# A hybrid decoder trunk in split fp32: each half-head's scores placed 24 or 28 steps behind the issue of their query and key loads instead of 3, and those loads 6 steps behind their stores instead of 1

## The chip, the cores and the metric

The kernel runs on one core of one Trainium2 chip. The metric is the device time of one execution in microseconds (us): 2202.98 us, the median of 3 runs (2202.58 to 2203.88). Lower is better.

## The reference

One decoder layer (sequence 1024, width 2048), float32 in and out. One input projection feeds eight differential-attention heads and eight recurrent blocks; their gated outputs go through one output projection.

```
h = rms_norm(x, norm_gain);  proj = h @ w_in          # [1024, 2048] @ [2048, 6144]
q, k, v, g_attn, xr, g_rec = split(proj)
q, k = rope(q), rope(k)                               # 8 heads x 2 maps x 64
...                                                   # per 128 query rows, causal:
  p = softmax(mask(q_m . k_m / 8))  for m = 0, 1
  w = p[0] - lam * p[1];  o = w @ v                   # 8 heads x 128
o = rms_norm(o, subln_gain) * silu(g_attn)
r = rg_lru(causal_conv(xr)) * silu(g_rec)             # 8 blocks x 128, a scan over the sequence
x = x + concat(o, r) @ w_out;  out = rms_norm(x, final_gain)
```

## The kernel before

The sequence is worked off in two halves of 512 tokens (`b`, and `l` where attention speaks of the half). Every dense product is done in three matmuls on a high and a low part of each operand (`triple`, L363: weight high by data high, weight high by data low, weight low by data high). A weight tile of 128 x 512 is loaded by SP, rounded into its high part on ACT (L169) and subtracted into its low part on POOL or DVE (L170); it serves four triples. The units of a half are taken in the order of `UNITS` (L56): a head is four projections of 16 triples each (two for queries and keys, one for values, one for the gate), a recurrent block two.

All other work runs beside this stream as Python generators in `Slots` (L64). Their clock, `now`, advances by one step after each triple, so a step is 3 matmuls of PE, and `yield n` puts the rest of a generator n steps further down the stream. That sets the program's order by hand; the framework's scheduler then moves single instructions on each engine's queue. Each engine, SP included, takes its own queue in order.

The path that the change touches is that of a head's queries and keys:
- `head` (L422) multiplies the two projections with the rotary tables on DVE; `rope` (L459) adds them, splits the results into high and low parts, and 4 steps later stores four tiles to `fs` in HBM (L155, `fs<-b`, each 4x32x512, 256 KB). One step later it marks the head ready.
- `loader` (L608) then calls `head_load` (L584), which reads the head back in another layout, all on SP: the new half's two key tiles (128x512) and four query tiles, each of 64 rows fetched twice (128x1x512). In the second half of the sequence it also loads the first half's two key tiles and the two value tiles `vs`.
- `scores` (L656) waits until the head is in `hd`, then 3 steps more, and runs `score` (L617) for four blocks of 128 queries, 10 steps apart. One block is, for each of the two maps, L632 (query high) and L633 (query low) into the accumulator `sw`, twice where the keys exceed 512; then the masked maximum on DVE (L637), the exponentials on ACT (L644), and the weighted difference on DVE (L652). `weighted` (L676) transposes the result on PE (L755) and multiplies it with the values (L777 to L780).

The tiles `b` are 89 slots that are given out in the order in which they come free (`alloc`, `rel`); a load into a slot waits for the slot's last reader.

Of the kernel before, what the change touches and what calls it, by code (L numbers as in the profile page):

```python
# [55 lines left out]
UNITS = ("h0", "h1", "r0", "h2", "r1", "h3", "r2", "h4", "r3", "h5", "r4", "h6", "h7", "r5", "r6",  # L56
         "r7")
ORDER = (0, 1, 2, 3, 4, 8, 9, 10, 11, 12, 5, 6, 13, 14, 7, 15)
SCORE_STEP = 2
SCORE_PACE = (4, 4)  # L60
TURN_PACE = 2
# [2 lines left out]
class Slots:  # L64


    def __init__(self):
        self.now = 0
        self.seq = 0
        self.tasks = []  # L70
# [36 lines left out]
class Trunk:  # L107
    def __init__(self, ctx, tc, io):
        self.tc = tc
        self.nc = tc.nc  # L110
        self.io = io
        e = ctx.enter_context
        self.cst = e(tc.tile_pool(name="cst", bufs=1))
        self.dram = e(tc.tile_pool(name="scr", bufs=1, space=bass.MemoryType.DRAM))
        self.bp = e(tc.tile_pool(name="buf", bufs=1))
        self.ps = e(tc.tile_pool(name="ps", bufs=1, space=bass.MemoryType.PSUM))
        self.tr, self.av, *self.dense = [
            self.ps.tile([P, HALF], F32, name=f"pq{i}") for i in range(4)]
        self.swide = [self.ps.tile([P, 1024], F32, name=f"sw{i}") for i in range(2)]
        self.n = 0  # L120
        self.sl = Slots()
        self.free = deque(range(NB))
        self.wide = [self.bp.tile([P, 1024], F32, name=f"wide{i}") for i in range(5)]
        self.avbusy = self.trbusy = False
        self.cur = self.phase = 0
        self.rsb, self.sin, self.cos, self.tabs, self.Y = {}, {}, {}, {}, {}
        self.fs, self.vsc, self.vnow, self.gate, self.rgate, self.msc = {}, {}, {}, {}, {}, {}
        self.ready, self.hd, self.es = set(), {}, {}
        self.scored, self.flipped, self.weighed = [], 0, 0

    def nm(self, s):
# [110 lines left out]
    def weights(self):  # L242
        io = self.io
        for b in range(2):
# [7 lines left out]
            yield from (io["w_in"][u, g] for u in us for g in range(4))  # L252
            yield from (io["w_out"][cg, kt] for cg in range(4) for kt in ORDER)

# [204 lines left out]
    def rope(self, b, h, ts):  # L459
        nc = self.nc  # L460
        t1, t2, t3, t4 = ts
        self.tt(t1.f, t1.f, t2.f, ALU.subtract)
        self.tt(t3.f, t3.f, t4.f, ALU.add)
        yield 1
        self.split(t1.f, t2, t1)
        self.split(t3.f, t4, t3)
        yield 4
        fs = self.dram.tile([4, 4, 32, HALF], F32, name=self.nm("fs"))
        for i, t in enumerate((t2, t4, t1, t3)):
            self.load(fs[:, i], t.f)  # L470
        self.rel(*ts)
        self.fs[h, b] = fs
        yield 1
        self.ready.add(("q", h, b))

    def values(self, b, h, vt):
# [107 lines left out]
    def head_load(self, h, l):  # L584
        k, q, v = [], [], []
        for c in range(l + 1):
            ks = []
            for m in range(2):
                kk = self.allocr()
                self.load(kk.f, self.fs[h, c][2 + m].rearrange("i r c -> (i r) c"))  # L590
                ks.append(kk)
            k.append(ks)
        for i in (0, 2):
            for m in range(2):
                t = self.allocr()
                src = self.fs[h, l][m, i:i + 2].rearrange("i r c -> (i r) c")
                self.load(t.f, src.unsqueeze(0).broadcast_to([2, 64, HALF]))
                q.append(t)
        if l:
            vs = []  # L600
            for d in self.vsc[h]:
                t = self.allocr()
                self.load(t.f, d)
                vs.append(t)
            v.append(vs)
        self.hd[h, l] = (k, q, v)

    def loader(self):  # L608
        for l in range(2):
            for h in range(NH):  # L610
                while (("q", h, l) not in self.ready or 8 * l + h - self.weighed > 1
                       or len(self.free) < FREE_HEAD):
                    yield 1
                self.head_load(h, l)
                yield 1

    def score(self, h, l, j, p0, es):  # L617
# [8 lines left out]
        for m in range(2):  # L626
            st = self.swide[m]
            for c in range((cols + 511) // 512):
# [4 lines left out]
                nc.tensor.matmul(o, lhsT=q[2 + m].r[:, qs], rhs=kk, start=False, stop=True)  # L633
        yield SCORE_STEP
        for m in range(2):
# [4 lines left out]
        nc.vector.tensor_scalar_mul(mx, mx, -(QK ** -0.5))  # L640
        yield SCORE_STEP
        p1 = self.wide[3]
        for m, p in enumerate((p0, p1)):
            nc.scalar.activation(p[:, :cols], self.swide[m][:, :cols], AF.Exp, scale=QK ** -0.5,  # L644
                                 bias=mx[:, m:m + 1], accum_out=sm[:, m:m + 1])
        yield SCORE_STEP
        nc.vector.tensor_tensor(out=es[:, j:j + 1], in0=sm[:, 0:1], in1=sm[:, 0:1], op=ALU.mult)
# [8 lines left out]
    def scores(self):  # L656
        n = 0
        for l in range(2):
            for h in range(NH):
                while (h, l) not in self.hd:  # L660
                    yield 1
                yield 3
                es = self.cst.tile([P, 4], F32, name=self.nm("es"), tag="es", bufs=4)
                self.es[h, l] = es
                for j in range(4):
                    while n - 2 * self.flipped > 3:
                        yield 1
                    p0 = self.wide[(0, 1, 2, 4)[n % 4]]
                    n += 1
                    yield from self.score(h, l, j, p0, es)  # L670
                    self.scored.append(p0)
                    yield SCORE_PACE[l]
                k, q, v = self.hd[h, l]
                self.rel(*q, *(t for ks in k for t in ks))
# [118 lines left out]
    def outputs(self, b):  # L793
# [10 lines left out]
        for cg in range(4):  # L804
            for i, kt in enumerate(ORDER):
                while cg == 0 and len(raws) + len(mixes) < min(KT, i + 5):
                    raws.append(self.mix(ORDER[len(raws) + len(mixes)], b))
                while cg == 0 and len(mixes) < min(KT, i + 2):
                    x, hi, lo = raws.popleft(), self.allocr(), self.allocr()
                    mixes[ORDER[len(mixes)]] = (hi, lo)  # L810
                    self.split(x.f, hi, lo)
# [55 lines left out]
            self.rel(y)  # L867

    def run(self):
        engines = {mybir.EngineType.PE, mybir.EngineType.SP}  # L870
        if True:
            self.consts()
            for gen in (self.stream(), self.loader(), self.scores(), self.weighted()):
                self.sl.spawn(gen)
            for b in range(2):
                for name in UNITS:
                    (self.head if name[0] == "h" else self.rec)(b, int(name[1]))
                self.final(b)
                self.outputs(b)
# [58 lines left out]
```

## Time and profile before

| what | value |
|---|---|
| median of 3 runs | 2202.98 us |
| the profiled execution | 2201.42 us |
| its span, first to last instruction | 2199.6 us |
| PE busy | 1739.8 us, 79% |
| POOL, ACT, DVE busy | 858.7, 793.6, 761.4 us |
| mean granted TensorE clock | 0.883 |
| DMA, mean rate | 108 GB/s |

The profile gives each engine's busy time and, for each group of instructions, the idle time just before them and what ended it. TensorE has two clock levels, 1.2 and 2.4 GHz; a granted clock of 1.00 in a stretch is the higher, 0.50 the lower. Idle time of an engine costs something only where the end of the program hangs on that engine.

### The profile page before, as it was taken

Reading aid. Unit: us, or ns where it says so; the run is one execution under the profiler, and the core shown is the slowest. Engines: PE = TensorE matmul, PEld = TensorE weight load, DVE = VectorE, ACT = ScalarE, POOL = GpSimd, SP = SyncE. Lnnn points to the kernel's source line nnn. Section 1 sums busy time; section 2 is a strip of 40 time slices with the busy share of each in tenths; the row PEclk is TensorE's granted clock in tenths of the full one; section 3 lists DMA queues with packets and bytes.
Section 4 is the critical chain, followed back from the end, with each engine's and each line's share of the span. In section 5 each row is a group of like instructions: output and inputs, shape, how many; then the busy total and the mean of one; then the engine's idle time right before and its main releaser. Section 6 shows DMA issues by size and latency. Waiting matters only on the chain. (4 is left out here: it accounts for less than half of the span.)

```text
span 2199.6 us, 22066 instructions
## 1 busy us (share of the span) xinstructions
PE 1739.8 (79%) x7716; PEld 1409.8 (64%) x7716; DVE 761.4 (35%) x1333; ACT 793.6 (36%) x1383; POOL 858.7 (39%) x710
## 2 busy tenths in 40 slices
PE   7568695959595869989957786959595958689996
PEld 5357474748484657778846675848484847577885
DVE  8334141515141335740223433324232424346001
ACT  6215151515151326642413342424251513266221
POOL 7313433424251325766613142415151513256560
PEclk9779897979797979999979897979797979799998
DMA  5423323233322234523723142423232323245422
GB/s 200 136 78 99 108 82 105 85 102 99 100 91 87 87 120 150 163 67 122 255 81 107 56 131 64 120 69 116 74 115 74 103 84 99 91 131 188 117 78 77
DMA packets 131503, 237.03 MB, mean 108 GB/s; under 512 B 13248, under 2 KB 17472, under 8 KB 131392
## 3 DMA queue, kind: packets, MB, share of 16 engines
q1 hardware_dynamic: 131392, 235.63, 34.2%
q8 instruction: 60, 0.98, 0.2%
q14 instruction: 51, 0.42, 0.1%
HBM read 197.83 MB, written 37.75 MB: 107 GB/s over the span
## 5 line engine op out<-in xcount | busy, mean ns | idle before, releaser
L367 PE MATMUL pq<-b,b 128*128 128x512 f32 x4512 | 1162.4, 410 | 17.2 <-ACT b L169 8.0
L170 POOL TENSOR_TENSOR b<-b,b 128x512 fp32r<-128x512 f32 x504 | 678.2, 1359 | 990.3 <-ACT b L169 706.6
L367 PEld LDWEIGHTS pq<-b,b 128*128 128x128 f32 x4512 | 877.5, 199 | 195.1 <-ACT b L169 8.5
L169 ACT CAST b<-b 128x512 fp32r<-128x512 f32 x592 | 349.7, 618 | 848.5 <-PE pq L367 219.6
L632 PE MATMUL sw<-b,b 128*128 128x512 f32 (+2 forms) x192 | 78.1, 408 | 278.1 <-DMA b<-fs 277.8
L173 DVE TENSOR_TENSOR b<-pq,b 128x512 f32<-128x512 f32 x113 | 75.1, 687 | 525.9 <-PE pq L367 434.6
L632 PEld LDWEIGHTS sw<-b,b 128*128 128x128 f32 x192 | 42.2, 220 | 296.3 <-issue 169.1
L637 DVE CUSTOM_DVE_ANT_0 sw<-sw,mask 128x128 f32<-128x128 f32 (+7 forms) x128 | 96.6, 770 | 376.2 <-PE sw L633 375.9
L826 PE MATMUL pq<-b,b 128*128 128x512 f32 x768 | 198.2, 393 | 5.0 <-DVE wide L173 5.0
L826 PE MATMUL sw<-b,b 128*128 128x512 f32 x768 | 196.3, 391 | 0.0
L826 PEld LDWEIGHTS pq<-b,b 128*128 128x128 f32 x768 | 144.9, 189 | 37.0 <-DVE wide L173 5.9
L826 PEld LDWEIGHTS sw<-b,b 128*128 128x128 f32 x768 | 145.3, 189 | 30.5
L173 POOL TENSOR_TENSOR b<-b,b 128x512 f32<-128x512 f32 (+1 forms) x98 | 129.4, 1325 | 89.8 <-ACT b L548 31.6
L633 PE MATMUL sw<-b,b 128*128 128x512 f32 (+2 forms) x192 | 77.1, 407 | 103.0 <-DMA b<-fs 103.0
L633 PEld LDWEIGHTS sw<-b,b 128*128 128x128 f32 x192 | 40.8, 212 | 126.8 <-DMA b<-fs 120.5
L644 ACT ACTIVATE wide<-sw,mx 128x128 f32<-128x128 f32 (+7 forms) x128 | 93.8, 738 | 67.0 <-DVE mx L640 66.2
L170 DVE TENSOR_TENSOR b<-b,b 128x512 fp32r<-128x512 f32 x88 | 92.1, 1071 | 32.5 <-ACT b L169 25.7
L169 ACT CAST b<-pq 128x512 fp32r<-128x512 f32 x16 | 9.4, 587 | 253.3 <-PE pq L483 253.3
L763 POOL MEMSET b<- 128x128 f32 x64 | 12.9, 205 | 185.0 <-PE pq L367 181.3
L764 ACT CAST b<-pq 128x512 fp32r<-128x512 f32 (+1 forms) x80 | 43.4, 542 | 108.5 <-PE pq L755 108.5
L765 DVE TENSOR_TENSOR b<-pq,b 128x512 fp32r<-128x512 f32 (+1 forms) x80 | 50.7, 634 | 45.1 <-ACT b L764 37.7
L755 PE MATMUL pq<-ident,wide 128*128 128x128 f32 x288 | 52.1, 286 | 17.6 <-DVE wide L652 16.8
(130 smaller groups left out, 1345.3 us busy)
## 6 DMA issues: line engine op xcount, KB each, us to landing
b<-w_in SPq DMA_DIRECT2D x384, 256.0 KB
b<-w_out SPq DMA_DIRECT2D x128, 256.0 KB
b<-fs SPq DMA_DIRECT2D x112, 256.0 KB
fs<-b SPq DMA_DIRECT2D x64, 256.0 KB
b<-xt SPq DMA_DIRECT2D x32, 256.0 KB
ms<-b SPq DMA_DIRECT2D x32, 256.0 KB
b<-ms SPq DMA_DIRECT2D x32, 256.0 KB
wide<-x SPq DMA_DIRECT2D x20, 256.0 KB
```

What stands on the lines that cost most here:

```text
L169: self.nc.scalar.copy(hi.r, x)
L170: (eng or self.nc.vector).tensor_tensor(out=lo.r, in0=x, in1=hi.f, op=ALU.subtract)
L173: (eng or self.nc.vector).tensor_tensor(out=out, in0=a, in1=b, op=op)
L367: self.nc.tensor.matmul(acc, lhsT=x.r[:, s], rhs=y.r, start=kt == 0 and j == 0, stop=kt == KT - 1 and j == 2)
L632: nc.tensor.matmul(o, lhsT=q[m].r[:, qs], rhs=kk, start=True, stop=False)
L633: nc.tensor.matmul(o, lhsT=q[2 + m].r[:, qs], rhs=kk, start=False, stop=True)
L637: nc.vector.tensor_tensor_reduce(out=s, in0=s, in1=self.mask[:, 896 - off:896 - off + cols], scale=1.0, scalar=NEG, op0=ALU.add, op1=ALU.m ...
L644: nc.scalar.activation(p[:, :cols], self.swide[m][:, :cols], AF.Exp, scale=QK ** -0.5, bias=mx[:, m:m + 1], accum_out=sm[:, m:m + 1])
L755: nc.tensor.transpose(self.tr[:, c:c + P], ws[qi][:, kb * P:(kb + 1) * P], self.ident)
L764: nc.scalar.copy(wh.r[:, first:], self.tr[:, first:])
L765: nc.vector.tensor_tensor(out=wl.r[:, first:], in0=self.tr[:, first:], in1=wh.f[:, first:], op=ALU.subtract)
L826: nc.tensor.matmul(accs[t], lhsT=x.r[:, s], rhs=z.r, start=i == 0 and j == 0, stop=i == KT - 1 and j == 2)
```

## The change

The scores of a head no longer start 3 steps after the scheduler of generators sees the loads issued; they start when the step counter has reached the step of the loads' issue plus 24 in the first half, 28 in the second. `rope` marks a head ready 6 steps after its stores instead of 1. A variable that was not used goes away.

```diff
 ORDER = (0, 1, 2, 3, 4, 8, 9, 10, 11, 12, 5, 6, 13, 14, 7, 15)
+SCORE_LEAD = (24, 28)
 SCORE_STEP = 2
...
-        self.ready, self.hd, self.es = set(), {}, {}
+        self.ready, self.hd, self.es, self.loaded = set(), {}, {}, {}
...
         self.fs[h, b] = fs
-        yield 1
+        yield 6
         self.ready.add(("q", h, b))
...
         self.hd[h, l] = (k, q, v)
+        self.loaded[h, l] = self.sl.now
...
                 while (h, l) not in self.hd:
                     yield 1
-                yield 3
+                while self.sl.now < self.loaded[h, l] + SCORE_LEAD[l]:
+                    yield 1
...
     def run(self):
-        engines = {mybir.EngineType.PE, mybir.EngineType.SP}
```

Lines behind the first one move down by one to three: L367, L632 and L633 become L368, L634 and L635.

PE's queue at the first scores of head 3 in the first half, before (`pq` are the projections' accumulators, `sw` those of the scores). The last matmul of the head's second projection, `pq_68<-b_410,b_2187`, stands 50 rows ahead of the first row that writes `sw`:

```order
L367 MATMUL pq_69<-b_410,b_2261 128x512
L367 MATMUL pq_68<-b_108,b_2288 128x512
L632 MATMUL sw_70<-b_2305,b_2309 128x256
L367 MATMUL pq_68<-b_109,b_2288 128x512
L367 MATMUL pq_68<-b_108,b_2289 128x512
L367 MATMUL pq_68<-b_114,b_2288 128x512
L632 MATMUL sw_71<-b_2307,b_2311 128x256
L367 MATMUL pq_68<-b_115,b_2288 128x512
L367 MATMUL pq_68<-b_114,b_2289 128x512
L367 MATMUL pq_68<-b_120,b_2288 128x512
L633 MATMUL sw_70<-b_2305,b_2313 128x256
```

The same scores in the changed program:

```order
L368 MATMUL pq_69<-b_126,b_2389 128x512
L368 MATMUL pq_69<-b_127,b_2389 128x512
L368 MATMUL pq_69<-b_126,b_2390 128x512
L634 MATMUL sw_70<-b_2326,b_2330 128x256
L635 MATMUL sw_70<-b_2326,b_2334 128x256
L634 MATMUL sw_71<-b_2328,b_2332 128x256
L635 MATMUL sw_71<-b_2328,b_2336 128x256
L368 MATMUL pq_69<-b_154,b_2409 128x512
L368 MATMUL pq_69<-b_155,b_2409 128x512
```

Before, 49 projection matmuls lay between the second projection's end and the first score, and others between the scores; now 108 projection matmuls (36 triples) and four transposes lie ahead, and the four scores stand together. In the second half the scores move the same way, from 44 projection matmuls behind the second projection to 120 (40 triples).

SP's queue at the same head, before (`fs` is the scratch in HBM, the rows with 128x1x512 are query tiles, those with 128x512 from `fs` key tiles):

```order
L155 DMA b_2504<-w_a 128x128
L155 DMA fs_2292<-b_2104 4x32x512
L155 DMA fs_2292<-b_2106 4x32x512
L155 DMA fs_2292<-b_2103 4x32x512
L155 DMA fs_2292<-b_2105 4x32x512
L155 DMA b_2504<-w_x 128x128
L155 DMA b_2309<-fs_2292 128x1x512
L155 DMA b_2311<-fs_2292 128x1x512
L155 DMA b_2305<-fs_2292 128x512
L155 DMA b_2307<-fs_2292 128x512
L155 DMA b_2313<-fs_2292 128x1x512
L155 DMA b_2315<-fs_2292 128x1x512
```

And in the changed program:

```order
L156 DMA b_2449<-w_x 128x128
L156 DMA fs_2292<-b_2039 4x32x512
L156 DMA fs_2292<-b_2038 4x32x512
L156 DMA fs_2292<-b_2041 4x32x512
L156 DMA fs_2292<-b_2040 4x32x512
L156 DMA b_2529<-w_in 128x512
L156 DMA b_2330<-fs_2292 128x1x512
L156 DMA b_2332<-fs_2292 128x1x512
L156 DMA b_2326<-fs_2292 128x512
L156 DMA b_2328<-fs_2292 128x512
L156 DMA b_2334<-fs_2292 128x1x512
L156 DMA b_2336<-fs_2292 128x1x512
```

Stores and loads keep their order on SP; one weight load now stands between them where a small gate weight stood, and the two stores of high parts are no longer the first two. SP's loads thus do not move against its stores; the scores on PE move against both.

## Rows read from the trace of the kernel before

**Rows 1.** The page's parts 1 and 5: busy time of the engines, and the groups of the projections' matmuls, of the weights' subtraction on POOL and of their rounding on ACT (line engine op, out<-in, count | busy us, mean ns of one | idle time just before, what ended most of it).

```profile
PE 1739.8 (79%) x7716; PEld 1409.8 (64%) x7716; DVE 761.4 (35%) x1333; ACT 793.6 (36%) x1383; POOL 858.7 (39%) x710
...
L367 PE MATMUL pq<-b,b 128*128 128x512 f32 x4512 | 1162.4, 410 | 17.2 <-ACT b L169 8.0
L170 POOL TENSOR_TENSOR b<-b,b 128x512 fp32r<-128x512 f32 x504 | 678.2, 1359 | 990.3 <-ACT b L169 706.6
...
L169 ACT CAST b<-b 128x512 fp32r<-128x512 f32 x592 | 349.7, 618 | 848.5 <-PE pq L367 219.6
```

**Rows 2.** The waits of PE, longest total first (engine, tile, line <- what it waited for: us in total, times, longest).

```profile
PE sw L632 <- DMA b<-fs: 277.8, 24, 19.2
PE sw L633 <- DMA b<-fs: 103.0, 32, 5.3
PE pq L755 <- DVE wide L652: 16.8, 20, 3.1
```

**Rows 3.** The timeline of PE around head 3 of the first half (start us, us, engine line op, out<-in, count [idle before <- releaser]).

```profile
333.64 22.83 PE L367 MATMUL pq<-b,b 128*128 128x512 f32 x100
375.09 0.55 PE L632 MATMUL sw<-b,b 128*128 128x256 f32 x1 [18.62 <-DMA b<-fs]
...
381.08 0.58 PE L633 MATMUL sw<-b,b 128*128 128x256 f32 x1 [2.66 <-DMA b<-fs]
...
386.41 0.58 PE L633 MATMUL sw<-b,b 128*128 128x256 f32 x1 [3.68 <-DMA b<-fs]
```

**Rows 4.** The timeline of DVE after that head's second projection.

```profile
345.40 1.29 DVE L173 TENSOR_TENSOR b<-pq,b 128x512 f32<-128x512 f32 x2 [9.59 <-PE pq L367]
```

**Rows 5.** The timeline of SP in the same stretch; a row's length is the time from its first issue to the end of its last.

```profile
348.39 3.14 SPq L155 DMA_DIRECT2D fs<-b  x4
...
357.29 14.84 SPq L155 DMA_DIRECT2D b<-fs  x6
372.18 6.99 SPq L155 DMA_DIRECT2D b<-w_in  x4
```

**Rows 6.** The chain that ended last, for head 3 of the second half (start us, us, what).

```profile
1399.74 19.09 PE pq L367 x84
...
1424.21 12.63 DMA fs<-b
...
1436.92 2.61 SPq L155
...
1440.85 19.39 DMA b<-fs
```

**Rows 7.** The timeline of PE for that head.

```profile
1399.50 29.29 PE L367 MATMUL pq<-b,b 128*128 128x512 f32 x128
1443.31 0.76 PE L632 MATMUL sw<-b,b 128*128 128x512 f32 x1 [14.51 <-DMA b<-fs]
...
1448.38 0.80 PE L632 MATMUL sw<-b,b 128*128 128x512 f32 x1 [3.03 <-DMA b<-fs]
...
1455.22 0.50 PE L633 MATMUL sw<-b,b 128*128 128x512 f32 x1 [2.52 <-DMA b<-fs]
...
1460.29 0.79 PE L633 MATMUL sw<-b,b 128*128 128x512 f32 x1 [3.54 <-DMA b<-fs]
...
1461.80 4.19 PE L367 MATMUL pq<-b,b 128*128 128x512 f32 x9
```

**Rows 8.** Windows (from:to us, length, then busy us and count of PE, weight loads, DVE, ACT and POOL; granted clock, share of the 16 DMA engines, GB/s): the first and the last are stretches in which PE works at the higher clock, the second, fifth and sixth are the low-clock stretches around the heads of rows 3 and 7, and in the third and fourth head 0's loads move and little else.

```profile
345.30:356.50 11.20, 11.17 (x50) 8.92 (x48) 4.43 (x7) 2.34 (x4) 2.57 (x2) 1.00 0.29 82
359.90:390.70 30.80, 9.27 (x24) 6.80 (x25) 1.90 (x8) 4.12 (x9) 4.42 (x4) 0.50 0.33 109
99.00:104.00 5.00, 0.00 (x0) 0.00 (x0) 0.00 (x0) 0.00 (x0) 0.00 (x0) 0.50 0.13 51
113.00:118.00 5.00, 1.51 (x5) 1.20 (x5) 0.53 (x3) 0.12 (x1) 0.00 (x0) 0.50 0.13 51
...
1431.70:1452.20 20.50, 5.87 (x13) 4.21 (x14) 0.69 (x1) 1.75 (x3) 3.97 (x4) 0.50 0.25 85
1455.60:1465.90 10.30, 6.76 (x21) 5.20 (x20) 3.36 (x8) 2.67 (x6) 1.28 (x1) 0.50 0.16 47
...
1010.00:1090.00 80.00, 80.00 (x354) 66.26 (x354) 15.26 (x30) 33.20 (x65) 49.51 (x40) 1.00 0.55 179
```

**Rows 9.** The timeline of PE at the first two heads, 0 and 1 of the first half.

```profile
72.97 4.02 PE L367 MATMUL pq<-b,b 128*128 128x512 f32 x9 [7.73 <-DVE b L173]
...
105.01 0.55 PE L632 MATMUL sw<-b,b 128*128 128x256 f32 x1 [17.34 <-DMA b<-fs]
...
116.61 0.58 PE L633 MATMUL sw<-b,b 128*128 128x256 f32 x1 [3.49 <-DMA b<-fs]
...
158.37 0.55 PE L632 MATMUL sw<-b,b 128*128 128x256 f32 x1 [6.30 <-DMA b<-fs]
...
169.82 0.58 PE L633 MATMUL sw<-b,b 128*128 128x256 f32 x1 [4.83 <-DMA b<-fs]
```

**Rows 10.** The waits of ACT for weight loads (as in rows 2).

```profile
ACT b L169 <- DMA b<-w_in: 57.8, 14, 19.9
```

**Rows 11.** The timeline of SP at head 1 of the first half (as in rows 5).

```profile
131.41 3.13 SPq L155 DMA_DIRECT2D fs<-b  x4
...
140.32 14.76 SPq L155 DMA_DIRECT2D b<-fs  x6
```

## The prediction

> **What bounds the kernel now.** I read the page's busy times and groups first, then PE's waits, then the timelines of PE, DVE and SP around one head of each half, then the chain. PE works 1739.8 us of the span of 2199.6 [rows 1], and of its idle time 277.8 + 103.0 = 380.8 us end with the landing of a transfer `b<-fs`, a head's queries or keys; the next cause has 16.8 [rows 2]. PE has nothing to do in these waits: its queue is in order and the score stands at its front. So PE is the bound, and the loads of 16 heads take 23.8 us each from it.
>
> One head in detail. PE stops at 356.47, the end of its 100 matmuls in 22.83 us, which is 0.228 us each [rows 3]. The head's second projection ended 49 matmuls earlier, at 356.47 - 11.2 = 345.3, and DVE takes it up at 345.40 [rows 4]. Call that moment T. SP stores at T + 3.1, begins to load at T + 12 and has issued its last load at T + 26.8 [rows 5]. PE's three waits end at T + 29.8, T + 35.8 and T + 41.1 [rows 3]: two query tiles land 5.3 apart. In the second half the projection ends at 1418.83, the third and fourth stores land 12.63 after 1424.21, and the last load lands 19.39 after 1440.85, at T + 41.4 [rows 6]; PE's waits end at T + 24.5, 29.6, 36.4 and 41.5 [rows 7]. The stall is thus what is left of a chain of 41 us after the few steps that PE had beside it.
>
> The chain is one of transfers, not of issue. While head 0's loads move and little else, the 16 DMA engines are 0.13 busy and carry 51 GB/s, where a stretch of weight loads has 0.55 and 179 [rows 8]: about 2 of 16 engines work. A 256 KB tile at 51 GB/s takes 5.1 us, the distance of the landings.
>
> **The change, part by part.**
>
> Loads 6 steps behind stores. SP waited for the stores' landing anyway: it had issued the stores by T + 6.2 and began the loads at T + 12 [rows 5]. Five more steps are 15 matmuls, 3.4 us, and lie inside that wait. The weight load that now stands between them waits for a slot that PE frees 8 triples after T, 5.5 us, also inside. The first load now needs the third store too; this can cost up to the 2.6 us between two stores' landings, but the engines are busy with the fourth store until then. I put the part at nothing, with T + 41 to stand; bounds are 3 us less (the chain without its waits for single stores) and 3 more (one store, one weight load).
>
> Scores later. In the first half the scores stand 108 matmuls behind T instead of 49 to 58: 24.6 us and four transposes, so PE comes to them at T + 24.9. It waits until T + 29.8 for a key tile, until T + 35.8 for the low part of the first map's queries, and until T + 41.1 for the second map's; three score matmuls of some 0.35 us lie between. That leaves 41.1 - 24.9 - 1.0 = 15.2 us of the 18.62 + 2.66 + 3.68 = 25.0 [rows 3]. In the second half 120 matmuls stand ahead, 27.4 us and the transposes, so PE comes at T + 27.6, when the first query tile has landed. It waits from there to T + 36.4 and to T + 41.5, and does about 1.8 us of score matmuls in between: 12.1 us are left of 14.51 + 3.03 + 2.52 + 3.54 = 23.6 [rows 7].
>
> Heads 0 and 1 of the first half differ. Head 0's projections end before 72.97, and its loads land until 116.61 [rows 9]; with 24.9 us to the scores, 116.6 - 97.9 - 1.0 = 17.7 are left of 23.8. Head 1's second projection ends 32 triples behind 72.97, at 95, but its stores stand on SP behind the loads of head 0. From its stores to its last landing it took 169.82 - 131.41 = 38.4 us [rows 9, 11]; put behind 118 that gives 156.4. PE is 40 triples behind 117 by then, 27.3 us and some 4 of scores and low clock, at 149: 7 us are left of 16.4.
>
> Stall in all: 17.7 + 7 + 6 x 15.2 + 8 x 12.1 = 213 us instead of 381, a gain of 168.
>
> Clock. The wait also costs clock. In the low-clock stretch of head 3 PE was busy 9.27 us at 0.50, in that of the second half 5.87 + 6.76 = 12.6 [rows 8]. There nine matmuls take 4.19 us, 0.47 each [rows 7], twice the 0.228 of rows 3, so half of the busy time is lost: 4.6 and 6.3 us a head. Afterwards only the scores and the 4.3 to 5.6 us until the clock is back stand in it, some 5.5 and 7 us, which lose 2.8 and 3.5. Gain 8 x 1.8 + 8 x 2.8 = 37.
>
> What is added. Each head's maxima, exponentials and transposes now follow the landing with 10 steps between blocks. PE waited for such a result 20 times for 16.8 us, 3.5 at most [rows 2]. Bounds are nothing and 3.5 a head, 56 in all; I take 0.5 a head, half of what a head has now (16.8 over 16), so 8 us. Weights: behind the loads SP issues none before T + 26.9 [rows 5], but in the new order the first of these serves projection matmuls 228 places behind T, 52 us, so nothing.
>
> Sum against the profiled execution of 2201.4 us, which stands 1.6 below the median: 2201.4 - 168 - 37 + 8 = **2004 us**.
>
> **The rivals.**
>
> *The chain is shorter than the lead, and the stall goes.* If the last load landed by T + 25, PE would lose neither the 381 us nor the low clock after it, 8 x 4.6 + 8 x 6.3 = 87: 2201.4 - 381 - 87 + 8 = 1741. Needed is a chain 16 us shorter with the same transfers on the same two engines; the 5 us between landings speak against it. The Trainium skill, page "DMA: Bandwidth & Descriptors", section "Anatomy of one DMA — SWDGE (gpsimd) path", gives 2.0 us and bytes over 436 GB/s for one DMA (of the other issue path); by it four stores and then six loads of 256 KB would land about 13 us after T + 3, and this rival would come true. The trace disagrees with its 41 us. The same page, "Why a DMA increments its semaphore by 16 and not by 1", has the number of engines follow from the outermost dimension, here 2 for a tile fetched twice, and the share of 0.13 agrees with that.
>
> *The wait moves to the weights.* PE now uses weights for 25 us and more while SP issues almost none; a row of `w_in` serves four triples, 2.7 us. Were one row too few loaded ahead, PE would stop 2.7 us before the scores and wait for a load that lands behind the queries, at T + 41, and for its rounding and subtraction, 0.6 and 1.4 us [rows 1], to about T + 44. That is 44 - 22.2 = 21.8 us a head in the first half and 44 - 24.9 = 19.1 in the second, 6.6 and 7.0 more than in the sum: 2004 + 109 = 2113. Against it: the new order places the first use of such a load 52 us behind T.
>
> *Slower: the first exponentials are caught behind weight casts on ACT.* In ACT's new order a head's first exponentials stand behind casts of weights that SP issues behind the head's loads. PE's next scores overwrite the same `sw`, 30 matmuls or 6.8 us later, so a wait beyond that stops PE. ACT has waited for such loads 14 times, up to 19.9 us [rows 10]. At 19.9 on every head PE would lose 13.1 x 16 = 210: 2214. It decides from 19.1 us a head on, where 12.3 x 16 takes up the gain of 197. Against it: the average of rows 10 is 4.1.
>
> *The change does not do what it says.* The order of the changed program shows the scores where they should be, so I give this nothing.
>
> **How the numbers follow.** Forecast 84%, stall gone 4%, weights 8%, slower 4%. The forecast's own range: 3 us of chain either way are 48 us, and the transposes' bounds are 8 less and 48 more; 1950 to 2070 holds that, without both ends coming together, in about nine of ten of its cases. That is some 76%; the weights case reaches into the range's upper part for smaller sums, which makes about 80. 0.2%, 4.4 us, is what a measurement of this kernel can tell from no change. All cases but the last are faster by more than that, with a rest for two small effects that cancel: faster 0.95, same 0.01, slower 0.04.
>
> **What would show it.** In the changed profile PE's waits for `b<-fs` should sum to about 213 us, mostly in two or three pieces a head: near 5 each in the first half, near 9 and 4 in the second. From the second projection's end to the last landing it should still be 41 us. The granted clock should rise from 0.883 to about 0.93, and the mean of the L367 group (410 ns, [rows 1]) fall towards 400. The forecast is wrong if that chain is not 41 us long, if PE's waits for weights or for L652 grow to tens of us, or if ACT's casts hold the exponentials back.

## The result and the profile after

The changed kernel takes 2131.62 us, the median of 4 runs (2128.7 to 2133.4); the kernel before took 2202.78 us beside it (2200.41 to 2203.88). The ratio is 0.9675, with a 95% interval of 0.9663 to 0.9686. That is 71 us faster where 197 were forecast, and 62 us above the upper end of the range.

The page of the changed kernel, parts 1 and 5, for [rows 1]; the ACT row is the rounding of the weights:

```profile
PE 1723.7 (81%) x7716; PEld 1406.6 (66%) x7716; DVE 790.8 (37%) x1333; ACT 809.4 (38%) x1395; POOL 853.8 (40%) x710
...
L368 PE MATMUL pq<-b,b 128*128 128x512 f32 x4512 | 1146.3, 407 | 32.8 <-DVE b L171 13.9
...
L170 ACT CAST b<-b 128x512 fp32r<-128x512 f32 x592 | 349.3, 617 | 1007.3 <-DMA b<-w_in 432.8
```

The waits of PE, for [rows 2] (engine, tile, line <- what it waited for: us in total, times, longest):

```profile
PE sw L635 <- DMA b<-fs: 131.7, 22, 11.5
PE pq L758 <- DVE wide L654: 58.3, 23, 5.0
PE pq L758 <- DVE b L768: 57.1, 5, 27.2
PE sw L634 <- DMA b<-fs: 26.0, 6, 5.6
PE pq L737 <- DVE hs L734: 25.1, 2, 24.1
PE pq L545 <- ACT b L170: 20.4, 11, 5.5
PE pq L780 <- ACT b L767: 16.5, 1, 16.5
PE pq L368 <- DVE b L171: 13.9, 2, 12.5
```

The waits for `b<-fs` fell from 380.8 to 131.7 + 26.0 = 157.7 us, more than forecast. But PE's idle time, span less busy time, fell only from 2199.6 - 1739.8 = 459.8 to 2129.0 - 1723.7 = 405.3 us. The rest of PE's idle time has grown from 79 to 248 us. In the list above it is waits for DVE and ACT. Some have a longest near 25 us: these are single events and not a toll on every head.

The heads that have no other head within 64 steps (2 to 5) went as forecast. The timelines of DVE and PE around head 3 of the first half, for [rows 3, 4] (start us, us, engine line op, out<-in, count [idle before <- releaser]):

```profile
341.75 1.29 DVE L174 TENSOR_TENSOR b<-pq,b 128x512 f32<-128x512 f32 x2 [6.55 <-PE pq L368]
```

```profile
371.34 0.43 PE L634 MATMUL sw<-b,b 128*128 128x256 f32 x1 [4.67 <-DMA b<-fs]
377.48 0.58 PE L635 MATMUL sw<-b,b 128*128 128x256 f32 x1 [5.71 <-DMA b<-fs]
...
382.54 0.58 PE L635 MATMUL sw<-b,b 128*128 128x256 f32 x1 [4.26 <-DMA b<-fs]
```

With T at 341.75, PE comes to the scores at 371.34 - 4.67 = T + 24.9, and the waits end at T + 29.6, T + 35.7 and T + 40.8: the chain is as long as before, and 14.6 us of wait are left, where the sum had 15.2. At head 3 of the second half, for [rows 7], T is 1378.67:

```profile
1415.47 0.80 PE L635 MATMUL sw<-b,b 128*128 128x512 f32 x1 [9.32 <-DMA b<-fs]
...
1420.56 0.80 PE L635 MATMUL sw<-b,b 128*128 128x512 f32 x1 [3.44 <-DMA b<-fs]
```

12.8 us there, where the sum had 12.1, ending at T + 36.8 and T + 41.9.

Now a place where the sum failed, heads 0 and 1 of the second half, which are 64 steps apart. SP, ACT, DVE and PE:

```profile
1142.67 3.13 SPq L156 DMA_DIRECT2D fs<-b  x4
1145.89 2.71 SPq L156 DMA_DIRECT2D b<-w_in  x1
1151.54 13.23 SPq L156 DMA_DIRECT2D b<-fs  x6
1164.81 10.73 SPq L156 DMA_DIRECT2D b<-w_in  x6
```

The third of those six rows by itself:

```profile
1172.54 0.60 SPq L156 DMA_DIRECT2D b<-w_in  x1
```

```profile
1155.16 0.62 ACT L170 CAST b<-b 128x512 fp32r<-128x512 f32 x1 [0.34 <-PE pq L368]
1183.64 0.62 ACT L170 CAST b<-b 128x512 fp32r<-128x512 f32 x1 [27.86 <-DMA b<-w_in]
1184.17 0.58 ACT L767 CAST b<-pq 128x512 fp32r<-128x512 f32 x1
...
1188.44 0.62 ACT L170 CAST b<-b 128x512 fp32r<-128x512 f32 x1 [0.27 <-PE pq L368]
```

```profile
1184.84 0.69 DVE L768 TENSOR_TENSOR b<-pq,b 128x512 fp32r<-128x512 f32 x1 [28.70 <-issue]
```

```profile
1185.58 1.12 PE L758 MATMUL pq<-ident,wide 128*128 128x128 f32 x4 [27.20 <-DVE b L768]
```

Read them from the bottom. PE's transposes (L758) of head 0 wait 27.2 us for the accumulator that DVE's subtraction (L768) must empty. DVE waits for ACT's cast of the transposes before (L767). ACT has that cast's data, but stands for 27.9 us in front of it, in the rounding of a weight row of `w_in` (L170). That row is the third of the six behind the loads of head 1: SP issues it at 1172.54, 16.8 us after ACT has begun to wait for it (1183.64 - 27.86 = 1155.78). Of its 16 parts 14 have landed at 1176.9, the last two at 1182.3 and 1183.6; ahead of it went head 1's queries, on two engines. "Issue" as DVE's releaser means that the profile saw no single event; ACT's L767 is the row just before it.

The program's order on ACT shows one thing more. The rows that SP issued at 1145.89, 1164.81 and 1172.03 are rounded after the held one, the first of them at 1188.44, though it had landed at 1158.3. PE's first use of the held row stands 198 matmuls behind the transposes that wait. So ACT stands for a row that is not the next one needed; the scheduler placed its rounding there.

There are five such places, all at the first or the last two heads of a half (0 and 1, 6 and 7), which are 64 steps apart: before 163.48 (16.5 us), 760.52 (24.2), 1185.58 (27.2), 1742.55 (12.5) and 1823.44 (27.2), 107.6 us together. ACT comes to the held row 8.4, 9.3, 16.8, 6.3 and 16.7 us before SP issues it, and at each of the five it rounds at least one row that was issued earlier only afterwards. What stands behind the held rounding is the work of the head before in four of them (its transposes' casts, at 760.52 its last scaling, L733), and the head's own transposed values at 1742.55. At the other heads ACT is held as well, 19 to 29 us each, but there PE has to wait for its scores anyway, and little of it shows.

### The profile page after: what moved, and what is told of

It is laid out like the page before. It is cut to its first block, busy times and chain, and to the rows that moved or that the text cites. A ratio compares the mean times of both kernels' runs of the same rounds, so it can differ in the third digit from the quotient of the medians.

```text
span 2129.0 us, 22112 instructions
## 1 busy us (share of the span) xinstructions
PE 1723.7 (81%) x7716; PEld 1406.6 (66%) x7716; DVE 790.8 (37%) x1333; ACT 809.4 (38%) x1395; POOL 853.8 (40%) x710
## 4 chain that ended last, share of the span: by engine, by line
PE 40%; DMA 20%; DVE 14%; issue 9%; SPq 7%; ACT 5%; POOL 4%; ACTq 0%; POOLq 0%; DVEq 0%
PE pq L368 19%; DMA b<-w_in 8%; DMA fs<-b 7%; PE pq L829 7%; PE sw L829 7%; SPq L156 7%; DMA b<-fs 3%; POOL b L171 2%; DVE b L174 2%; ACT b L170 2%; DVE b L171 1%; PE pq L758 1%; POOL b L174 1%; DVE sw L639 1%; DVE b L533 1%
## 5 line engine op out<-in xcount | busy, mean ns | idle before, releaser
L368 PE MATMUL pq<-b,b 128*128 128x512 f32 x4512 | 1146.3, 407 | 32.8 <-DVE b L171 13.9
L171 POOL TENSOR_TENSOR b<-b,b 128x512 fp32r<-128x512 f32 x504 | 676.0, 1355 | 1054.5 <-ACT b L170 676.0
L368 PEld LDWEIGHTS pq<-b,b 128*128 128x128 f32 x4512 | 867.7, 197 | 210.6 <-DVE b L171 15.6
L170 ACT CAST b<-b 128x512 fp32r<-128x512 f32 x592 | 349.3, 617 | 1007.3 <-DMA b<-w_in 432.8
L829 PE MATMUL pq<-b,b 128*128 128x512 f32 x768 | 198.9, 394 | 4.5 <-DVE wide L174 4.0
L635 PE MATMUL sw<-b,b 128*128 128x512 f32 (+2 forms) x192 | 74.1, 393 | 131.7 <-DMA b<-fs 131.7
L829 PEld LDWEIGHTS sw<-b,b 128*128 128x128 f32 x768 | 145.7, 190 | 30.6
L174 POOL TENSOR_TENSOR b<-b,b 128x512 f32<-128x512 f32 (+1 forms) x98 | 126.8, 1295 | 64.6 <-DVE b L740 26.5
L758 PE MATMUL pq<-ident,wide 128*128 128x128 f32 x288 | 56.4, 306 | 115.3 <-DVE wide L654 58.3
L635 PEld LDWEIGHTS sw<-b,b 128*128 128x128 f32 x192 | 39.9, 208 | 145.1 <-DMA b<-fs 139.7
L455 DVE SCALAR_TENSOR_TENSOR b<-b,b 128x512 f32<-128x512 f32 x32 | 30.8, 963 | 268.8 <-ACT b L453 268.8
L758 PEld LDWEIGHTS pq<-ident,wide 128*128 128x128 f32 x288 | 38.3, 156 | 135.2 <-DVE wide L654 68.6
L171 DVE TENSOR_TENSOR b<-b,b 128x512 fp32r<-128x512 f32 x88 | 92.4, 1070 | 48.1 <-ACT b L170 45.2
L768 DVE TENSOR_TENSOR b<-pq,b 128x512 fp32r<-128x512 f32 (+1 forms) x80 | 50.9, 636 | 158.8 <-ACT b L767 101.4
L634 PE MATMUL sw<-b,b 128*128 128x512 f32 (+2 forms) x192 | 71.6, 378 | 31.4 <-DMA b<-fs 26.0
L767 ACT CAST b<-pq 128x512 fp32r<-128x512 f32 (+1 forms) x80 | 43.3, 541 | 108.5 <-PE pq L758 106.1
L174 DVE TENSOR_TENSOR wide<-pq,wide 128x512 f32<-128x512 f32 x12 | 8.2, 690 | 166.2 <-PE pq L829 166.2
```

The lines of the kernel that those rows point to most:

```text
L170: self.nc.scalar.copy(hi.r, x)
L171: (eng or self.nc.vector).tensor_tensor(out=lo.r, in0=x, in1=hi.f, op=ALU.subtract)
L174: (eng or self.nc.vector).tensor_tensor(out=out, in0=a, in1=b, op=op)
L368: self.nc.tensor.matmul(acc, lhsT=x.r[:, s], rhs=y.r, start=kt == 0 and j == 0, stop=kt == KT - 1 and j == 2)
L634: nc.tensor.matmul(o, lhsT=q[m].r[:, qs], rhs=kk, start=True, stop=False)
L758: nc.tensor.transpose(self.tr[:, c:c + P], ws[qi][:, kb * P:(kb + 1) * P], self.ident)
```

## The experiments

Theory A: the missing gain is lost where a weight row's late landing holds ACT, which takes its queue in order, while other work of PE's next steps stands behind. Theory B: it is lost in the chain of maxima, exponentials and combination that now follows a late landing in 10-step distances. Each figure is a median, beside the kernel before at 2200.6 to 2202.7 us on the same chip.

### 1. The lead alone

```diff
-        yield 6
+        yield 1
         self.ready.add(("q", h, b))
```

> The scores 24 or 28 steps behind the issue of their loads, the loads again 1 step behind their stores. Theory A (the missing gain is lost in ACT's casts of weight rows that SP issued behind a head's loads; ACT works in order, and the previous head's casts of transposed scores stand behind them) expects what the changed kernel does, since SP waits for the stores' landing in any case: 2131 us, within 15, PE's waits for b<-fs near 158 us and five waits of 12 to 27 us where two heads are 64 steps apart. Theory B (the missing gain is lost in the chain of maxima, exponentials and the combination of maps that now follows a late landing 10 steps apart) expects the same within 15. If the 6 steps do matter, over 2150 or under 2110.

Measured: 2104.29 us (ratio 0.9562, 0.9534 to 0.959), 27 us *faster* than the whole change. The waits for `b<-fs` are longer, the others shorter:

```profile
PE sw L635 <- DMA b<-fs: 163.8, 26, 12.1
PE sw L634 <- DMA b<-fs: 55.9, 6, 10.2
PE pq L758 <- DVE wide L654: 42.4, 19, 5.8
PE pq L726 <- ACT b L723: 33.9, 3, 17.2
```

163.8 + 55.9 = 219.7 us, 62 more than with the 6 steps; the scores come 5 steps sooner. But what PE waits for at the close heads is 10.4, 16.2 and 17.2 us at three places instead of 107.6 at five. So the part that shortens the named stall lengthens the run. Both theories had expected no difference, and both missed. At heads 1 and 7 of the two halves ACT is held 15 to 25 us here, and 24 to 28 us with the 6 steps.

### 2. The six steps alone

```diff
-SCORE_LEAD = (24, 28)
+SCORE_LEAD = (3, 3)
```

> The loads 6 steps behind their stores, the scores again 3 steps behind the loads. The scores come 5 steps later than in the kernel before, 15 matmuls of 0.228 us, 3.4 us a head. Both theories: PE's waits for b<-fs fall by up to 55 us from 381, to about 326; no wait of over 10 us for another cause; 2147 to 2190 us, near 2150 if the waits shrink by all of it.

Measured: 2194.28 us (0.9957 to 0.998 times the kernel before): nearly nothing, where 55 us less waiting were expected. At head 3 PE reaches its first score 11.07 us and 49 projection matmuls behind T in both kernels, and waits 24.8 us instead of 25.0. The scores were written 5 steps later, but the scheduler had put them there already. Written and placed order are two things; the expectation took the first for the second.

### 3 and 4. The query loads on 16 engines, with the long lead and with the short one

```diff
-                self.load(t.f, src.unsqueeze(0).broadcast_to([2, 64, HALF]))
+                self.load(t.f[:64], src)
+                self.load(t.f[64:], src)
```

The second kernel has the order of the kernel before as well (`SCORE_LEAD = (3, 3)`, `yield 1`).

> The changed kernel with each broadcast query load replaced by two plain loads of 64 rows, so that 16 engines instead of 2 carry them. Estimate: the last landing moves from T + 41 to about T + 27 (first half) and T + 32 (second), and the rows of w_in issued behind land at once. Theory A: PE's waits for b<-fs fall from 158 to under 60 us, ACT's waits for w_in from 433 to under 100, and the five waits of 12 to 27 us (108 us in all) go: about 1880 us, 1840 to 1920. Theory B: the waits for b<-fs fall likewise, but the waits of the transposes for wide (58 us) and the long ones remain: about 2010, 1980 to 2040.

> The kernel before (scores 3 steps behind the loads, loads 1 step behind the stores) with each query load as two plain loads of 64 rows on 16 engines. If the chain of transfers is as limited by 2 engines as both theories say, the stall of 23.8 us a head falls by some 9 to 14 us: 2202 - 16 x 9 to 14 = 1980 to 2060 us, with a little clock on top. Theory A expects few waits for weights here and nothing else new; theory B the same. If the chain is limited by something else (the stores, the latency of a transfer), 2150 to 2200.

Measured: 1838.85 us with the lead (ratio 0.8356, 0.8321 to 0.839) and 1917.31 without it (0.8712, 0.8687 to 0.8738). The first is 41 us below theory A's figure, 1 us below its range, and 171 below theory B's figure. The second is 63 us below the range that was expected: the two engines had cost more than was put down to them. While head 3's loads move, the 16 DMA engines are 0.65 busy and carry 214 GB/s; for head 0 in [rows 8] it was 0.13 and 51. The window and SP's rows of the kernel with the lead:

```profile
305.00:315.00 10.00, 10.00 (x46) 8.25 (x45) 1.38 (x2) 1.94 (x4) 4.79 (x6) 1.00 0.65 214
```

```profile
305.69 7.14 SPq L156 DMA_DIRECT2D b<-fs  x10
312.93 1.00 SPq L156 DMA_DIRECT2D vs<-b  x2
313.99 28.83 SPq L156 DMA_DIRECT2D b<-w_in  x8
```

Ten loads leave SP in 7.1 us where six took 14.8 [rows 5], and weight rows follow at once. The last query tile lands at T + 23.5 (T is 291.69 here) instead of T + 41. With the lead, PE's and ACT's longest waits are now:

```profile
PE pq L759 <- DVE wide L655: 55.6, 23, 5.0
PE pq L545 <- ACT b L170: 18.6, 11, 5.5
```

```profile
ACT b L170 <- DMA b<-w_in: 201.6, 38, 11.7
```

The five long waits are gone and the waits for `b<-fs` sum to 4.2 us. ACT still waits 201.6 us for rows, twice what A had expected, but never over 11.7 us for one, and no long wait of PE hangs on it. The waits for `wide` stay at 55.6 us, 39 more than in the kernel before: theory B names a real cost, about a third of the 127 us that are missing, but it does not hang on a late landing.

That a load spreads by its outermost dimension is what the Trainium skill says (page "DMA: Bandwidth & Descriptors", section "Why a DMA increments its semaphore by 16 and not by 1": the largest number up to 16 that divides the slowest dimension of both sides). The traces agree: with each tile fetched twice the share was 0.13, about 2 of 16 engines; as 64 rows it is 0.65, over 10 of them at work on average.

### 5. The weight rows issued by ACT

```diff
-                self.load(raw.f, src[n])
+                self.nc.scalar.dma_start(raw.f, src[n])
```

> The changed kernel with the loads of weight rows issued by ACT instead of SP, so that they no longer stand in SP's queue behind a head's stores and loads; those are as before, on 4 and 2 engines. Theory A, first form (the rows are late because SP issues them late): ACT's waits for w_in of 20 to 29 us shrink to a few us and the five long waits of PE (108 us in all) go; at the heads that had no wait for b<-fs because PE came late to them, that wait is back, 4 or 5 heads with 12 to 15 us, so 2065 to 2095 us. Theory A, second form (the rows are late because their sixteenths share the two engines that carry the queries): ACT's waits stay above 10 us and the time stays above 2100. Theory B (the late chain of maxima, exponentials and combination): 2131, within 15.

Measured: 2092.34 us (0.9497, 0.947 to 0.9525), 39 us less than the change, within A's first form. ACT's waits for `w_in`, before and after this edit:

```profile
ACT b L170 <- DMA b<-w_in: 432.8, 39, 29.4
```

```profile
ACT b L170 <- DMA b<-w_in: 108.8, 30, 5.3
```

The transfers of the head are the same, on the same two engines, and the rows still use those two engines among their 16. So most of the lateness was SP's queue, not the shared engines. The edit also ends ACT's waiting for a row that is not yet issued, since ACT now issues it itself. But ACT is now also held under the name of `b<-fs`, as it never was in the change: 81.0 us before roundings and, with the transposes' casts (L767), five times for over 12 us (19.8, 15.9, 14.3, 13.5 and 12.5). At 1151.24, for one, a cast has stood behind an issue of ACT's own, which waited until 1150.8. The largest waits of PE for anything but `b<-fs` at the close heads are 12.5, 10.3, 8.2 and 7.2 us. One of the five absent waits for `b<-fs` came back (10.8 + 3.5 us), fewer than expected. A new wait is paid at four heads, 4.6 to 7.1 us: PE's projections wait for the accumulator of the transposed values (L368 for L171), whose cast stands on ACT behind its roundings and, now, behind its issues.

### 6. The transposes four steps later

```diff
-                    self.scored.append(p0)
                     yield SCORE_PACE[l]
+                    self.scored.append(p0)
```

> The changed kernel with a scored block handed to the transposes 4 steps after its combination is issued instead of at once; loads and lead as in the changed kernel. Theory B: PE's waits of the transposes for wide (58 us) fall under 15, 2080 to 2095 us. Theory A: these fall too, but the five long waits stay near 108 us, so 2080 to 2100 in all; where the casts stand differently in ACT's order a long wait may come or go, 20 us either way.

Measured: 2111.46 us (0.9584, 0.9556 to 0.9612), 16 us above theory B's figures and 11 above theory A's, within the 20 that A allowed for a long wait. The waits for `wide` fell to 37.8 us, not under 15, and those of the long kind stayed, at other lines:

```profile
PE pq L780 <- ACT b L767: 57.3, 3, 19.7
PE pq L758 <- DVE wide L654: 37.8, 13, 6.1
PE pq L545 <- ACT b L170: 23.1, 11, 3.2
PE pq L368 <- DVE b L171: 20.9, 1, 20.9
```

The six waits over 9 us at heads for another cause than a load (18.3, 20.9, 9.5, 14.8, 19.7, 19.3) sum to 102.5. Moving PE's work changes which instruction stands behind the held rounding, not that one does.

### 7 and 8. Query loads on 16 engines, a lead of 16 and 18 steps, and then the transposes later

```diff
-SCORE_LEAD = (24, 28)
+SCORE_LEAD = (16, 18)
...
-        yield 6
+        yield 1
```

The second kernel has the edit of experiment 6 as well.

> Query loads on 16 engines, scores 16 or 18 steps behind the issue of the loads, loads 1 step behind the stores. With 3 steps PE waited 8.7 us a head for b<-fs, which is 38 matmuls or 13 steps; 16 to 18 steps should cover it. Theory A: no wait for b<-fs above 2 us, no cast on ACT caught for 12 us, 1840 us or up to 20 less than with 24 and 28 steps (1839). If the lead itself costs by buffers held longer, 1810 to 1825; if it costs nothing, 1835 to 1845.

> The same with a scored block handed to the transposes 4 steps later. The waits of the transposes for wide, 48 to 56 us with split queries and 24 or 28 steps, should go: some 40 us less than the kernel without this edit, near 1795 us; under 15 us less if those waits only move to the products that follow.

Measured: 1879.25 and 1888.42 us, both slower than 1839 with the longer lead, so the expectations are missed. Of the first, PE waits 44.7 + 31.8 = 76.5 us for `b<-fs`, in pieces of 3 to 7 us, and only 5.7 us for `wide`. So a shorter lead leaves part of the landing uncovered, and the second edit had nothing left to win.

### 9. The close pair moved

```diff
-UNITS = ("h0", "h1", "r0", "h2", "r1",
+UNITS = ("h0", "r0", "h1", "h2", "r1",
```

> The changed kernel with the first pair of adjacent heads moved: heads 0 and 1 now have a recurrent unit between them, heads 1 and 2 have none. Theory A (a head's late weight row holds ACT while the casts of the head 64 steps ahead stand behind it) expects the long waits of PE near triples 120 and 1139 to move by about 96 triples, to near 216 and 1230, of 15 to 28 us each, with none over 13 us for another cause than b<-fs where they were; the last pair keeps its own; the time stays near 2131, within 25. Theory B, or any cause that lies in the beginning of a half, expects them to stay where they were.

Measured: 2142.80 us (0.9735, 0.9714 to 0.9755). The long waits moved along, to triples 213 and 1235, with one of 12.2 us at 1184, and the last pairs kept theirs; PE at the first two:

```profile
279.86 1.44 PE L737 MATMUL pq<-ident,hs 128*128 128x128 f32 x5 [24.88 <-DVE hs L734]
...
1306.66 1.11 PE L758 MATMUL pq<-ident,wide 128*128 128x128 f32 x4 [27.18 <-DVE b L768]
```

In the second half none over 4 us but for `b<-fs` is left around triple 1139. In the first, where none over 13 was expected, there are two, of 25.3 and 19.5 us at triples 96 and 149. The first has the same form with other work behind the rounding, the gates (L556, L557, L549) of the recurrent block that now follows head 0:

```profile
122.21 0.62 ACT L170 CAST b<-b 128x512 fp32r<-128x512 f32 x1 [25.88 <-DMA b<-w_in]
122.73 0.72 ACT L556 ACTIVATE b<-b,nsp 128x512 f32<-128x512 f32 x1
```

So it is not closeness of heads as such, but any work that PE needs soon and that stands behind the row.

### 10. A longer lead, with the slow loads

```diff
-SCORE_LEAD = (24, 28)
+SCORE_LEAD = (40, 44)
```

> The changed kernel with the scores 40 or 44 steps behind the issue of the loads. 16 steps are 48 matmuls, 10.9 us, so what PE waits for b<-fs at single heads falls from 15 and 13 us to 4 and 2: from 158 us to about 45. Theory A: the rows of w_in stay as late as they are, ACT's waits for w_in stay over 350 us, and PE now meets them at single heads too, in casts of scores, in products or in the projections: over 2070 us. Theory B, or if the late rows cost nothing beyond the pairs: 2131 - 113 = 2018, with some clock 2000 to 2030.

Measured: 2065.50 us (ratio 0.9383, 0.9361 to 0.9406). PE's waits for `b<-fs` fell to 3.8 us, and ACT still waits 270.7 us for `w_in`, where A had expected over 350, and 95.0 for `w_x`, 29.7 at most. In their place PE waits 83.1 us for `wide` (24.5 at most), 64.6 for a weight's subtraction (16.1), 33.3 for L723 and 32.6 for exponentials (27.4). The named stall is gone, and 66 of its 158 us are gained. That is 5 us below theory A's bound and 35 above theory B's range.

### 11 and 12. The way on

Query loads on 16 engines, and in the second half only, the transposes four steps later; the second kernel has a lead of 30 instead of 24 steps in the first half.

> The changed kernel with query loads on 16 engines (1839 us) and, in the second half only, a scored block handed to the transposes 4 steps later. The waits of 2.6 us of the second half's transposes go, 5 to 8 of them: 1815 to 1830 us; 1839 if the wait only moves to what follows.

> The same with 30 steps instead of 24 in the first half, so that a head's blocks meet the recurrent unit's gates on ACT and DVE elsewhere. If the 5.0 us waits of the first half's transposes come from that meeting they change, by up to 20 us in all in either direction: 1800 to 1845; if they come from the block's own chain they stay, and the time stays within 5 us of the kernel with 24.

Measured: 1825.93 us (1823.43 to 1829.48, 4 runs; ratio 0.8296, 0.8281 to 0.8311) and 1811.21 us (1809.43 to 1814.07; 0.8228, 0.8211 to 0.8244). Both lie in the ranges expected, and both beat both kernels; the last is 320 us faster than the changed kernel. Its PE is busy 92% of the span, its longest list entry is 30.8 us for `wide`, and no wait for `b<-fs` is among its first seven.

## Why the prediction was wrong

**The stall for the loads** was right in mechanism and nearly in size: T + 24.9, the chain of 41, and 15 and 12 us left a head came out within 1 us. Its total, 213, came out at 157.7, since five heads (1 and 7 of each half, 6 of the second) had no wait for `b<-fs`: PE came to them after a long wait of another kind. In the sum those had 7 + 15.2 + 3 x 12.1 = 58.5 us. So the 55 us by which the total is better are no gain: they are the other side of the long waits.

**"Weights: ... so nothing"** is the step that failed first. It asked when PE first needs a row that SP issues behind the head's loads, found 52 us, and stopped there. The row's first reader is not PE but ACT, whose rounding stands in ACT's queue long before, with casts behind it that PE needs at once. It cost the five waits, 107.6 us; it may have cost some of the 20.4 of L545, which no run separates. Net of the 58.5 us that the sum had at these five heads it is 49 us, the largest single term that was missed. Experiments 3, 5 and 9 show it: with rows issued elsewhere or with no slow loads ahead of them the waits shrink or go, and with the units in another order they move. No run rounds the rows in the order of their issue, so how much of the 49 us is the scheduler's order and how much the late landing stays open.

**The weights rival**, which rested on the same 52 us, did not come true: PE waited 8.4 us for a rounded weight (L368 for ACT's L170), and 8.0 before.

**The slower rival** had this mechanism and the wrong victim. It looked at the exponentials of the same head, which now stand clear of the held rounding, and priced them on every head. The victims are mostly the casts of the head before, where it is near, and a recurrent block's gates in experiment 9. So it came true at five heads of sixteen, with 12 to 27 us where it had 13.

**"What is added"**, 8 us within bounds of 0 to 56, measured 58.3 - 16.8 = 41.5 us for `wide`, and 9.8 more for L545. The waits for `wide` were inside the bounds, but 8 us, half of what a head had before, stood for 41.5. They go with the order of the steps and not with the landing: 16.8 and 17.2 us with the old order (slow loads and, in experiment 4, fast ones), 58.3 and 55.6 with the new (the change and experiment 3), 5.7 with a lead of 16 and 18 steps (experiment 7).

**The clock** was to give 37 us; PE's busy time fell by 16. The granted clock rose from 0.883 to 0.903 where 0.93 was forecast, and the mean of the L368 group fell from 410 to 407 ns. Summed over all of them, the low-clock stretches went from 517 to 415 us, with PE busy in them for 196 before and 167 after. At single heads of the first half the low clock comes twice now, once at the scores and once at the transposes' wait of 5.0 us; in the second half two short ones follow. Of the changed kernel, the first half's head 3 and the second half's, for [rows 8]:

```profile
371.50:388.60 17.10, 7.12 (x18) 5.32 (x18) 0.00 (x0) 3.35 (x5) 2.22 (x2) 0.50 0.37 120
422.70:429.50 6.80, 4.23 (x15) 3.57 (x15) 3.13 (x5) 0.59 (x1) 1.71 (x2) 0.50 0.25 80
1409.10:1426.20 17.10, 7.29 (x18) 5.61 (x19) 0.00 (x0) 2.31 (x4) 2.52 (x2) 0.50 0.28 90
1439.80:1443.20 3.40, 3.40 (x10) 2.51 (x9) 1.71 (x5) 3.34 (x7) 0.00 (x0) 0.51 0.09 13
1470.60:1474.00 3.40, 3.40 (x12) 2.71 (x11) 2.06 (x4) 0.59 (x1) 1.29 (x1) 0.50 0.23 63
```

PE is busy 7.12 + 4.23 = 11.4 us at the low clock at the first, where it was 9.3 and 5.5 were forecast; 14.1 at the second, where it was 12.6 and 7 were forecast. The step counted the stall's own low clock and not that of the waits that take its place.

Together: the profiled execution took 2130.8 us, 127 more than 2004. The stall came out 55 better. The other waits grew by 169 us (107.6 of the long kind, 41.5 for `wide`, 9.8 for L545, the rest small), 161 more than the 8. The busy time came out 21 worse: -55 + 161 + 21 = 127. So two steps failed. With the held rows alone the sum would have been 2004 + 49 = 2053, inside the range; with the transposes' 33 us beyond the 8 as well it is 2086, outside it; the clock's 21 and the smaller waits make up the rest.

That 5 steps more make the long waits so much longer (experiment 1 against the change) is read from the two orders on ACT, at heads 1 and 7 of the second half. Without the 6 steps ACT comes to the held row as SP issues it, at 1146.6 and 1779.0 against 1146.7 and 1779.9; it is the first row behind the loads, and the transposes' casts of the head before are done (its squares, L723, stand behind). With them ACT comes 17 us ahead of the issue, to the third row, and those casts stand behind. Why the scheduler orders them so stays open, and the runs give no rule by which to choose the steps.

## What to carry to other kernels

When a wait is moved, list for each transfer queued behind the slow one its *first* reader on any engine, and what stands behind that reader in its queue; the main engine's own need may lie 50 us later and say nothing. Check too whether that reader stands ahead of readers of rows that were issued earlier. A stall of one engine also hides every other queue that is held for as long, and those come to light when it goes. And look at the shape of the slow transfer before its place: two lines that put it on 16 engines gave 283 us with the old order, the reordering alone 71.

## What was not expected of the hardware

The slow loads hold their own issuer. In the change, at head 1 of the second half, six of them and the first weight row behind took SP from 1151.5 to 1171.9: that row's issue alone stood 7.1 us, while the shortest in the trace take 0.33. 14 of its 16 parts had landed at 1174.5, the last two at 1181.0 and 1182.3. With the queries on 16 engines (experiment 3, head 3) the issues took 0.3 to 0.7 us each.
